# Token-major latent attention in layer 0, and a stage's first weight splits ordered behind its norm

## The chip, the cores and the metric

The kernel runs on one core of a Trainium2 chip. The metric is the time of one execution in device microseconds, smaller is better. A core has five engines with a queue each: TensorE (PE, with its weight loads as PEld), VectorE (DVE), ScalarE (ACT), GpSimd (POOL) and SyncE (SP, which here only issues DMA transfers). Every queue runs in order: an instruction that waits holds all that stands behind it on the same engine.

## The reference

Two transformer blocks, one after the other, each of two layers, on 256 tokens of width 1024, in float32. Layer 0 of the first block also carries 256 context tokens. Its mixer joins a gated delta-rule recurrence over both directions with a latent attention of 8 heads; the joined 1024 features go through `w_out`. Cut to what the change touches:

```python
mod = (jax.nn.silu(c) @ w_mod[i] + b_mod[i])[:, None, :]      # 6 x 1024 columns: shift, scale, gate, twice
...
def blocked_attention(q, k, v, scale):
    ...
        s = jnp.einsum('bqkgd,bskd->bkgqs', q_i, k).astype(jnp.float32) * scale
        p = jax.nn.softmax(s, axis=-1).astype(v.dtype)
        return jnp.einsum('bkgqs,bskd->bqkgd', p, v)
...
    b_lat = blocked_attention(q_l, jnp.concatenate([k_c, k_l], 1), jnp.concatenate([v_c, v_l], 1), scale)
    y_lat = jnp.concatenate([a_lat, b_lat.reshape(b, s_len, -1)], -1) @ w_out
...
h = h + gt_m * rms_norm(y, g_post_mix[i])
f = swiglu(modulate(rms_norm(h, g_pre_ffn[i]), sh_f, sc_f), w_ffn_gate[i], w_ffn_up[i], w_ffn_down[i])
```

The context tokens attend to the context alone, the others to context and tokens. The modulation is computed for `c` and for `c_ctx`.

## The kernel before, in words

**Products with weights.** Every large product is done in three passes of a split format: a float32 matrix is cut into a high part and a remainder, and `mm3` (L553 to L556) adds high by high, high by low and low by high. For a weight, `Weights.load` and its sisters issue a DMA of a `[128, 2, 512]` piece (two contraction tiles by up to 512 columns, 512 KB) into a raw buffer `wraw`; `Weights.cut` has ScalarE write the high part `whi` (L270), and VectorE or POOL subtract to the low part `wlo`, one instruction for each of the two contraction tiles (L272). Which of the two does it is set by `W.turn`: a string with a letter for each of the stage's loads, V for VectorE and P for POOL; `turn("PPPP", "V")` gives the first four loads to POOL and the rest to VectorE. Raw buffers and part buffers rotate; a load waits until its buffer is free.

**The order of the work.** The program is written stage by stage, but when the kernel is built a planner lays out each engine's queue: it walks through a model of time and places what has its operands and buffers, what comes earlier in the program first. So work of a later part may be placed in the gaps of an earlier one. Buffers of a ring, and the eight accumulation banks of TensorE, are given out by kind with a fixed count each.

**Layer 0's mixer** has the banks `g` (3), `s` (2), `tp`, `po` and `gv` (one each). After the projections come the recurrence (`gdn_run`, over 8 pairs of direction and token tile, each two chunks of 64 tokens; its `gQ` operands are loaded by SP at L1172, its state is updated by POOL at L1207), `gdn_post`, the attention (`l0_mla`), and last six modulation chunks (`mod_chunk` for n = 4 to 9):

```python
with Pool(K, "mla", "right"):
    l0_mla(K, Om)
    for n in range(4, 10):
        mod_chunk(K, W, K.po, 0, n)
```

A modulation chunk takes a `gv` bank, multiplies four loads of `w_mod` into it (L370 the loads, L373 sixteen matmul instructions, 32 columns wide), copies the result to a row `mrow` on ScalarE (L375), takes a `gv` bank again for a closing product (L379 where the section is a gate, L386 elsewhere) and adds the bias on VectorE. Gate sections fetch bias and gain and store the gate row through POOL's queue.

**The attention before** is feature-major. For each of four head pairs and four tiles of 128 query tokens, `attend` makes scores, takes the row maximum (L674), the exponential with its row sum (L676), transposes the probabilities on TensorE (L679) and copies them (L682, L684). The product with the values has the values as stationary operand (128 by 64) and the probabilities streaming (L690), so that the output has features on partitions. The softmax sums are per token; `sums_row` takes the reciprocal of the sums broadcast to 128x128 (L698) and turns it by a matmul into the bank `gv` (L700). After the four tiles, L872 copies that bank and L873 multiplies. In `layer0` the result is split by features (four 128x512 splits).

**Where a stage begins.** A stage ends in `post_norm`: squares, a reciprocal root by Newton steps on VectorE (L319 to L323), the residual (L542), for some stages a product with a row of gains (L546), squares of the new residual on ScalarE (L514), and then `norm_tile`: the scaled identity `ndg` (L507) and matmuls with it that give the next stage's features (L489; L487 where there is no scaling), which are then split (L306, L307). The next stage's first weights are loaded and split meanwhile.

Of the kernel before, what the change touches and what calls it, by code (L numbers as in the profile page):

```python
# [10 lines left out]
F32 = mybir.dt.float32  # L11
# [92 lines left out]
def const(K, n):  # L104
    pack, a, b = COFF[n]
    return K.cst[pack][:, a:b]


def setup(K, tc, ctx, ins, out):
    K.nc = tc.nc  # L110
    K.tc = tc
    K.ins = ins
    K.out = out
    K.n = 0
    K.sb = ctx.enter_context(tc.tile_pool(name="sb", bufs=1))
    K.cur = K.sb
    K.dr = ctx.enter_context(tc.tile_pool(name="dr", bufs=1, space=DRAM))
    K.cst = {}
    K.open = []
    K.np = K.nu = 2  # L120
    K.c = lambda n: const(K, n)

# [77 lines left out]
def bank(K, kind):  # L200
    kind = K.alias.get(kind, kind)
    return K.ps[kind].tile([128, 512], F32, name=nm(K, kind), tag=kind, bufs=K.kinds[kind])
# [14 lines left out]
class Weights:  # L217
# [9 lines left out]
    def turn(self, pattern, then=None):  # L227


        self.first = pattern if then else ""  # L230
        self.rest = then or pattern
        self.nt = 0

    def engine(self):
# [33 lines left out]
    def cut(self, raw, hi, lo):  # L268
        e = self.engine()
        self.K.nc.scalar.copy(hi, raw)  # L270
        for k in range(raw.shape[1]):
            e.tensor_tensor(lo[:, k], raw[:, k], hi.bitcast(F32)[:, k], op=ALU.subtract)  # L272

# [229 lines left out]
def norm_tile(K, x, ss, coef, hi, lo, t):  # L503


    dg = cut(K, [128, 128], F32, "ndg", 2)
    K.nc.vector.tensor_scalar_mul(dg, K.ident, rstd2(K, ss, "n"))  # L507
    to_features(K, x, coef, hi, lo, t, dg)


def squares(K, h, ss, q, tag="yj"):

    j = cut(K, [128, 512], F32, tag, 1)
    K.nc.scalar.activation(j, h[:, q * 512:q * 512 + 512], AF.Square, accum_out=ss[:, q:q + 1])  # L514


def post_norm(K, G, hdst, after, sq=True, T=2, row=None, held=True):
# [6 lines left out]
    def consume(c, t, ps):  # L524
# [9 lines left out]
        if c == 1:  # L534
            r = rstd2(K, ss, "p")
            s2 = cut(K, [128, 2], F32, "hss", 4)
            h = x = hdst(t)
            if row is not None:
                x = cut(K, [128, D], F32, "xn", 2)
            for q in range(2):  # L540
                cq = slice(q * 512, q * 512 + 512)
                nc.vector.scalar_tensor_tensor(h[:, cq], ys[t, q], r, h[:, cq], op0=ALU.mult, op1=ALU.add)  # L542
                if sq:
                    squares(K, h, s2, q)
                if row is not None:
                    nc.vector.tensor_tensor(x[:, cq], h[:, cq], row[:, cq], op=ALU.mult)  # L546
            return lambda: after(t, s2, x)
# [117 lines left out]
def attend(K, score, v, po, rb, c, kinds=("s", "s", "tp", "tp")):  # L665
# [22 lines left out]
    for j in range(nj):  # L688
        for hh in range(2):
            nc.tensor.matmul(po[hh * 64:hh * 64 + 64, c:c + 128], v(hh, j), pts[hh][0][:, j * 128:(j + 1) * 128],  # L690
                             start=(j == 0), stop=(j == nj - 1))


# [94 lines left out]
def l0_mla(K, O):  # L788
# [50 lines left out]
    for pair in range(4):  # L839
        heads = {}  # L840
        for h in (2 * pair, 2 * pair + 1):
# [17 lines left out]
            heads[h] = (q1, q2, k1, k2)  # L859
        po, rb = bank(K, "po"), bank(K, "gv")  # L860
        for t in range(4):
            n = 256 if t < 2 else 512

            def score(pss):
                tk = slice(t * 128, (t + 1) * 128)
                for hh in range(2):
                    q1, q2, k1, k2 = heads[2 * pair + hh]
                    mm3(K, pss[hh][:, :n], q1[:, tk], q2[:, tk], k1[:, :n], k2[:, :n], True, True)
                    yield pss[hh][:, :n]
            attend(K, score, lambda hh, j: vt[:, j, pair * 128 + hh * 64:pair * 128 + hh * 64 + 64], po, rb, t * 128,  # L870
                   ("s", "g", "tp", "g") if late else ("s", "s", "tp", "tp"))
        nc.scalar.copy(O[:, pair, :], rb)  # L872
        nc.vector.tensor_tensor(O[:, pair, :], po, O[:, pair, :], op=ALU.mult)  # L873

# [860 lines left out]
def ple(K, W, i, xh, xl, pp, h, after=None, out=None, fill=None, row=None):  # L1735
# [4 lines left out]
    def consume(c, t, ps):  # L1740
# [7 lines left out]
        else:  # L1748
            if t not in sss:
                sss[t] = cut(K, [128, 2], F32, "yss", 4)  # L1750
                xs[t] = cut(K, [128, D], F32, "xn", 2)
            squares(K, h[t], sss[t], c)
            nc.vector.tensor_tensor(xs[t][:, cs], h[t][:, cs], row[:, cs], op=ALU.mult)
# [112 lines left out]
def layer0(K):  # L1866
# [18 lines left out]
    with Banks(K, {"acc": 5, "aux": 2, "gv": 1}):  # L1885
        with Pool(K, "tmp"):
# [3 lines left out]
            gdn_out(K, mh[:, 0:4], ml[:, 0:4])  # L1890
            for k in range(4):
                split(K, mh[:, 4 + k], ml[:, 4 + k], Om[:, k])
            K.dbg("gh", mh[:, 0:4])
# [14 lines left out]
        with Pool(K, "ff"):  # L1908
            hT = cut(K, [128, 22, 512])
            W.turn("PPPP", "V")  # L1910
            with Pool(K, "sg"):
# [47 lines left out]
def layer1(K, h):  # L1959
    nc = K.nc  # L1960
    ins = K.ins
    W = K.W
    K.px = opened(K, "w", "right")
    W.add(K.px, 1, 2)
    with Pool(K, "l1o"):
        load_const(K, "rest", K.cur)
        oh, ol = cut(K, [128, 8, 256], FR), cut(K, [128, 8, 256], FR)
        W.turn("PPPPPP", "V")
        with mix_banks(K), Pool(K, "l1"):
# [22 lines left out]
    with Pool(K, "ff"):  # L1992
        mh, ml = cut(K, [128, 22, 256], FR), cut(K, [128, 22, 256], FR)
        W.turn("VVVVPPPP", "V")
        with Pool(K, "sg"):
# [20 lines left out]
def second(K, h):  # L2016
# [10 lines left out]
    for i in range(2):  # L2027
        with Pool(K, "so"):
# [4 lines left out]
            W.add(K.px, 1, 2)  # L2033
            W.turn("PPPP", "V")
            with mix_banks(K), Pool(K, "sU"):
# [21 lines left out]
        with Pool(K, "ff"):  # L2057
            mh, ml = cut(K, [128, 32, 256], FR), cut(K, [128, 32, 256], FR)
            W.turn("VVVVPPPP", "V")
            with Pool(K, "sg"):  # L2060
# [110 lines left out]
```

## Time before, and its profile

| | |
|---|---|
| Median of 3 runs | 2217.39 us (2213.5 to 2222.52) |
| The profiled execution: time | 2211.2 us |
| Its span, first to last instruction | 2209.4 us |
| Mean granted TensorE clock | 0.936 of full speed |

A granted clock of 1.0 is 2.4 GHz and 0.5 is 1.2 GHz. Busy times of the engines overlap, so shares do not add up to one. An idle engine costs time only where the others wait for it. In the rows below, a line of a group gives line, engine, operation, output and inputs, shapes and count, then busy us and mean ns of one, then the idle time ahead of it and what ended that; a line in order of time begins with the start in us and the duration.

### The profile page before, as it was taken

Reading aid. Unit: us, or ns where it says so; the run is one execution under the profiler, and the core shown is the slowest. Engines: PE = TensorE matmul, PEld = TensorE weight load, DVE = VectorE, ACT = ScalarE, POOL = GpSimd, SP = SyncE. Lnnn points to the kernel's source line nnn. Section 1 sums busy time; section 2 is a strip of 40 time slices with the busy share of each in tenths; the row PEclk is TensorE's granted clock in tenths of the full one; section 3 lists DMA queues with packets and bytes.
Section 4 is the critical chain, followed back from the end, with each engine's and each line's share of the span. In section 5 each row is a group of like instructions: output and inputs, shape, how many; then the busy total and the mean of one; then the engine's idle time right before and its main releaser. Section 6 shows DMA issues by size and latency. Waiting matters only on the chain.

```text
span 2209.4 us, 31163 instructions
## 1 busy us (share of the span) xinstructions
PE 2035.4 (92%) x11656; PEld 1640.6 (74%) x11656; DVE 1319.9 (60%) x2737; ACT 921.9 (42%) x1612; POOL 241.2 (11%) x312
## 2 busy tenths in 40 slices
PE   6989898857999999979987999999899999989998
PEld 3777677614887877867656888898688879868886
DVE  5665566702678674463856556585675467566644
ACT  4533433402522223443435544455454345545532
POOL 2211112100100000020311000210200021020000
PEclk9999599957999999989969999999899999989999
DMA  8343300155267663222304557350566535145561
GB/s 273 91 111 82 116 11 16 59 170 171 85 204 234 223 200 105 96 88 67 96 20 152 154 151 241 111 145 20 162 198 188 158 117 162 44 153 167 185 190 68
DMA packets 186952, 291.90 MB, mean 132 GB/s; under 512 B 28472, under 2 KB 75704, under 8 KB 186800
## 3 DMA queue, kind: packets, MB, share of 16 engines
q1 hardware_dynamic: 172720, 272.54, 39.6%
q0 software_dynamic: 5472, 16.13, 2.2%
q10 hardware_dynamic: 8608, 1.23, 0.4%
q8 instruction: 92, 1.51, 0.3%
q14 instruction: 60, 0.49, 0.1%
HBM read 281.44 MB, written 8.41 MB: 131 GB/s over the span
## 4 chain that ended last, share of the span: by engine, by line
PE 81%; DVE 6%; DMA 5%; issue 3%; ACT 3%; POOL 1%; SPq 0%; ACTq 0%; DVEq 0%; POOLq 0%
PE acc L554 18%; PE acc L556 18%; PE acc L555 18%; PE s L554 2%; PE s L555 2%; PE s L556 2%; PE gv L373 2%; DMA wraw<-in_w_mod_dram 2%; PE po L1531 1%; PE tp L1531 1%; PE po L690 1%; PE tp L891 1%; PE aux L729 1%; PE aux L489 1%; PE g L1200 1%
## 5 line engine op out<-in xcount | busy, mean ns | idle before, releaser
L272 DVE TENSOR_TENSOR wlo<-wraw,whi 128x512 fp32r<-128x512 f32 (+4 forms) x772 | 483.1, 669 | 301.2 <-ACT whi L270 284.4
L270 ACT CAST whi<-wraw 128x1024 fp32r<-128x1024 f32 (+4 forms) x420 | 413.6, 990 | 491.2 <-PE acc L556 204.2
L554 PE MATMUL acc<-whi,u 128*128 128x512 f32 (+3 forms) x1320 | 511.5, 390 | 21.5 <-ACT whi L270 13.2
L555 PE MATMUL acc<-wlo,u 128*128 128x512 f32 (+3 forms) x1320 | 509.4, 388 | 0.8 <-DVE wlo L272 0.7
L556 PE MATMUL acc<-whi,u 128*128 128x512 f32 (+3 forms) x1320 | 507.9, 386 | 1.5 <-DVE u L307 1.5
L554 PEld LDWEIGHTS acc<-whi,u 128*128 128x128 f32 x1320 | 253.2, 192 | 72.7 <-ACT whi L270 15.1
L556 PEld LDWEIGHTS acc<-whi,u 128*128 128x128 f32 x1320 | 252.6, 191 | 51.7 <-DVE u L307 3.8
L555 PEld LDWEIGHTS acc<-wlo,u 128*128 128x128 f32 x1320 | 252.7, 192 | 51.2 <-DVE wlo L272 3.6
L554 PE MATMUL acc<-u,whi 128*128 128x512 f32 (+1 forms) x480 | 169.5, 360 | 1.8 <-ACT u L306 1.7
L556 PE MATMUL acc<-u,wlo 128*128 128x512 f32 (+1 forms) x480 | 170.1, 358 | 0.0
L555 PE MATMUL acc<-u,whi 128*128 128x512 f32 (+1 forms) x480 | 169.4, 355 | 0.2 <-DVE u L307 0.2
L272 POOL TENSOR_TENSOR wlo<-wraw,whi 128x512 fp32r<-128x512 f32 (+1 forms) x68 | 83.7, 1261 | 417.4 <-ACT whi L270 417.4
L432 DVE SCALAR_TENSOR_TENSOR msum<-mraw,u,msum 128x512 f32<-128x512 f32 x140 | 100.7, 745 | 12.8 <-DMA mraw<-in_w_mod_dram 11.7
L554 PEld LDWEIGHTS acc<-u,whi 128*128 128x128 f32 x480 | 89.5, 189 | 16.9 <-issue 2.6
L555 PEld LDWEIGHTS acc<-u,whi 128*128 128x128 f32 x480 | 90.4, 188 | 15.2 <-issue 1.7
L556 PEld LDWEIGHTS acc<-u,wlo 128*128 128x128 f32 x480 | 90.1, 188 | 15.1 <-issue 1.7
L307 DVE TENSOR_TENSOR u<-aux,u 128x512 fp32r<-128x512 f32 (+2 forms) x96 | 59.4, 632 | 44.0 <-ACT u L306 44.0
L373 PE MATMUL gv<-wraw,u 128*32 128x512 f32 x160 | 50.2, 900 | 32.2 <-DMA wraw<-in_w_mod_dram 24.6
L306 ACT CAST u<-aux 128x512 fp32r<-128x512 f32 (+2 forms) x96 | 50.4, 543 | 55.7 <-PE aux L729 35.8
L554 PE MATMUL acc<-whi,dxh 128*128 128x512 f32 x176 | 69.7, 396 | 1.9 <-ACT dxh L306 1.9
L555 PE MATMUL acc<-wlo,dxh 128*128 128x512 f32 x176 | 69.6, 396 | 0.0
L556 PE MATMUL acc<-whi,dxl 128*128 128x512 f32 x176 | 69.0, 396 | 0.0
(510 smaller groups left out, 3115.2 us busy)
## 6 DMA issues: line engine op xcount, KB each, us to landing
wraw<-in_w_up_dram SPq DMA_DIRECT2D x64, 512.0 KB, 4.2
wraw<-in_w_down_dram SPq DMA_DIRECT2D x64, 512.0 KB, 4.3
mraw<-in_w_mod_dram SPq DMA_DIRECT2D x56, 512.0 KB, 4.8
wraw<-in_w_ffn_down_dram SPq DMA_DIRECT2D x44, 512.0 KB, 3.8
wraw<-in_w_mod_dram SPq DMA_DIRECT2D x40, 512.0 KB, 4.8
wraw<-in_w_ffn_gate_dram SPq DMA_DIRECT2D x48, 256.0 KB, 3.0
wraw<-in_w_ffn_up_dram SPq DMA_DIRECT2D x48, 256.0 KB, 3.3
wraw<-in_w_ffn_gate_dram SPq DMA_DIRECT2D x20, 512.0 KB, 4.3
```

Source lines behind the costliest of these rows:

```text
L270: self.K.nc.scalar.copy(hi, raw)
L272: e.tensor_tensor(lo[:, k], raw[:, k], hi.bitcast(F32)[:, k], op=ALU.subtract)
L306: (hi_eng or nc.scalar.copy)(hi, src)
L307: nc.vector.tensor_tensor(lo, src, hi.bitcast(F32), op=ALU.subtract)
L373: nc.tensor.matmul(ps[32 * j:32 * j + 32, :], K.cl[:, g + k, :], raw[:, k, :], start=(g + k < 4), stop=(g + k >= 4))
L432: nc.vector.scalar_tensor_tensor(accs[s], raw[:, k, :], c, accs[s], op0=ALU.mult, op1=ALU.add)
L489: nc.tensor.matmul(ps[:, k * 128:(k + 1) * 128], xk, dg, start=True, stop=True)
L554: mm(ps, ah, bh, start=start, stop=False)
L555: mm(ps, ah, bl, start=False, stop=False)
L556: mm(ps, al, bh, start=False, stop=stop)
L690: nc.tensor.matmul(po[hh * 64:hh * 64 + 64, c:c + 128], v(hh, j), pts[hh][0][:, j * 128:(j + 1) * 128], start=(j == 0), stop=(j == nj - 1))
L1531: nc.tensor.matmul(ps[t][:, c * 128:c * 128 + 128], yp[:, c, t * 128 + j:t * 128 + j + 128] if j < 31 else ones, dg, start=(j == 0), stop= ...
```

## The change

Two things are done. Layer 0's attention becomes token-major: a new `attend_tok` uses the transposed probabilities as stationary operand and the values as streaming one, scales the output by the reciprocal of the two sums per token, and writes it with tokens on partitions; `layer0` turns the four token tiles by `out_features` (transposes on TensorE, then a split). The banks `po` and `gv` are no longer held over a head pair; `gv` isn't used by the attention at all. And at seven stage starts the turns with POOL become VectorE throughout; in their place `W.wait` orders the first weights' casts behind the square (on ScalarE) and their subtractions behind the scaled identity or the last residual operation (on VectorE) of a token tile. These are edges for the planner within one engine; they add no semaphore wait. `{0: 0, 4: 2}` means: loads from the 0th on go behind tile 0, from the 4th on behind tile 2, up to four loads past the last key.

```diff
@@ class Weights
     def turn(self, pattern, then=None):
+        self.behind = {}
...
+    def wait(self, chains):
+        self.behind = {n: self.K.chain[t] for n, t in chains.items()}
+
+    def order_of(self, ins, n, i):
+        at = [m for m in self.behind if m <= n]
+        if at and n < max(self.behind) + 4:
+            self.K.tc.add_manual_dep(ins.ins, self.behind[max(at)][i].ins.name, mybir.DependencyInfo(
+                mybir.DependencyClass.NoSync, mybir.DependencyReason.DATA), reason="norm first")
...
     def cut(self, raw, hi, lo):
-        e = self.engine()
-        self.K.nc.scalar.copy(hi, raw)
+        n, e = self.nt, self.engine()
+        self.order_of(self.K.nc.scalar.copy(hi, raw), n, 1)
         for k in range(raw.shape[1]):
-            e.tensor_tensor(lo[:, k], raw[:, k], hi.bitcast(F32)[:, k], op=ALU.subtract)
+            i = e.tensor_tensor(lo[:, k], raw[:, k], hi.bitcast(F32)[:, k], op=ALU.subtract)
+            if e is self.K.nc.vector:
+                self.order_of(i, n, 0)
@@ norm_tile
-    K.nc.vector.tensor_scalar_mul(dg, K.ident, rstd2(K, ss, "n"))
+    K.chain[t][0] = K.nc.vector.tensor_scalar_mul(dg, K.ident, rstd2(K, ss, "n"))
@@ post_norm
+            K.chain[t] = [v, a]        # last VectorE operation on the residual, last square
@@ new
+def attend_tok(K, pair, t, score, v, O, kinds=("s", "s", "tp", "tp")):
+    nc = K.nc
+    sm = cut(K, [128, 2], F32, "sm", 4)
+    pts = []
+    for hh in range(2):
...
+    po = bank(K, "po")
+    for hh in range(2):
+        pt, nj = pts[hh]
+        for j in range(nj):
+            nc.tensor.matmul(po[:, hh * 64:hh * 64 + 64], pt[:, j * 128:(j + 1) * 128], v(2 * pair + hh, j),
+                             start=(j == 0), stop=(j == nj - 1))
+    r = cut(K, [128, 2], F32, "rs", 4)
+    nc.vector.reciprocal(r, sm)
+    nc.vector.tensor_tensor(O.rearrange("p (h d) -> p h d", h=2), po[:, :128].rearrange("p (h d) -> p h d", h=2),
+                            bc(r, [128, 2, 64], 2), op=ALU.mult)
@@ l0_mla
-        po, rb = bank(K, "po"), bank(K, "gv")
...
-            attend(K, score, lambda hh, j: vt[:, j, pair * 128 + hh * 64:pair * 128 + hh * 64 + 64], po, rb, t * 128,
-                   ("s", "g", "tp", "g") if late else ("s", "s", "tp", "tp"))
-        nc.scalar.copy(O[:, pair, :], rb)
-        nc.vector.tensor_tensor(O[:, pair, :], po, O[:, pair, :], op=ALU.mult)
+            attend_tok(K, pair, t, score, lambda h, j: vt[:, j, h * 64:(h + 1) * 64],
+                       O[:, t, pair * 128:(pair + 1) * 128], ("s", "g", "tp", "g") if late else ("s", "s", "tp", "tp"))
@@ layer0
-            for k in range(4):
-                split(K, mh[:, 4 + k], ml[:, 4 + k], Om[:, k])
+            for t in range(4):
+                out_features(K, Om[:, t, :], mh, ml, 4, t)
@@ layer0, FFN
-            W.turn("PPPP", "V")
+            W.turn("V")
+            W.wait({0: 2})
@@ layer1, mixer
-        W.turn("PPPPPP", "V")
+        W.turn("V")
+        W.wait({0: 0, 4: 2})
@@ layer1, FFN (and the second block's FFN, twice)
-        W.turn("VVVVPPPP", "V")
+        W.turn("V")
+        W.wait({0: 0, 6: 1})
@@ the second block's mixer, twice
-            W.turn("PPPP", "V")
+            W.turn("V")
+            W.wait({0: 0})
```

The scores, maxima, exponentials and transposes of `attend_tok` are those of `attend`. The two products of `ple_product` keep their turn on POOL.

## Rows read from the trace of the kernel before

**Rows 1.** The page's first part: busy time, share of the span and instructions of each engine.

```profile
PE 2035.4 (92%) x11656; PEld 1640.6 (74%) x11656; DVE 1319.9 (60%) x2737; ACT 921.9 (42%) x1612; POOL 241.2 (11%) x312
```

**Rows 2.** Busy time of each engine in three stretches of layer 0's mixer. Columns: stretch, its length, busy us and instructions of PE, PEld, DVE, ACT, POOL, then granted TensorE clock, DMA share and GB/s.

```profile
185.00:434.00 249.00, 220.93 (x2401) 180.63 (x2401) 154.01 (x330) 94.23 (x220) 48.27 (x75) 0.86 0.19 52
434.00:515.00 81.00, 48.57 (x150) 13.60 (x149) 9.41 (x19) 8.45 (x15) 4.78 (x9) 0.58 0.52 167
515.00:535.00 20.00, 12.47 (x31) 8.24 (x31) 8.62 (x14) 6.86 (x8) 2.96 (x2) 0.67 0.63 218
```

**Rows 3.** The matmuls of line 373 from 255 to 560 us (durations as minimum, median, maximum, then first and last start), and what ended TensorE's idle time ahead of them (us, times).

```profile
L373 PE MATMUL gv<-wraw,u x96: 592/1061/1062, 434.0 to 511.4; 128*32 128x512 f32 x96
...
  DMA wraw<-in_w_mod_dram: 61.5, 22
```

**Rows 4.** The loads of `w_mod` in SP's queue in order of time (line 370), from 60 to 560 us.

```profile
179.79 1.56 SPq L370 DMA_DIRECT2D wraw<-in_w_mod_dram  x2
...
435.05 70.88 SPq L370 DMA_DIRECT2D wraw<-in_w_mod_dram  x22
```

**Rows 5.** The instructions that write or read the bank `gv` from 60 to 434 us, the attention's only.

```profile
L700 PE MATMUL gv<-const_id,rs x32: 272/275/582, 301.5 to 432.7; 128*128 128x128 f32 x32
...
L872 ACT COPY u<-gv x4: 579/588/592, 321.2 to 433.0; 128x512 f32<-128x512 f32 x4
```

**Rows 6.** TensorE in order of time in the stretch after the attention, runs of one line merged: two loads' matmuls, one load's, and a closing product.

```profile
433.96 1.07 PE L373 MATMUL gv<-wraw,u 128*32 128x512 f32 x8
...
439.19 1.05 PE L373 MATMUL gv<-wraw,u 128*32 128x512 f32 x4 [3.15 <-DMA wraw<-in_w_mod_dram]
...
473.70 1.87 PE L386 MATMUL gv<-const_id,mrow 128*128 128x2 f32 x8 [0.73 <-ACT mrow L375]
```

**Rows 7.** DMA issues from 434 to 515 us: count, KB each, median us from issue to landing.

```profile
wraw<-in_w_mod_dram SPq DMA_DIRECT2D x22, 512.0 KB, 4.1
```

**Rows 8.** Groups of instructions from 280 to 450 us: operations of the attention that the change takes out.

```profile
L698 DVE RECIPROCAL rs<-sm 128x128 f32<-128x128 f32 x16 | 15.2, 952 | 4.5 <-ACT p L676 4.1
...
L700 PE MATMUL gv<-const_id,rs 128*128 128x128 f32 x32 | 7.2, 308 | 0.0
...
L873 DVE TENSOR_TENSOR u<-po,u 128x512 f32<-128x512 f32 x4 | 2.8, 692 | 1.5 <-ACT u L306 1.2 <-PE po L690 0.3
```

**Rows 9.** First, TensorE in order of time: the attention's value product and what follows it, and the same for the second block's attention, which has probabilities as stationary operand. Then the weight loads of both, the second block's scaling and reciprocal, and the transposes that bring a recurrence output back to features.

```profile
318.96 1.09 PE L690 MATMUL po<-pt,u 128*64 128x128 f32 x14
319.98 0.66 PE L679 MATMUL tp<-const_id,p 128*128 128x128 f32 x4
...
1545.85 1.00 PE L1660 MATMUL po<-u,pt 128*128 128x64 f32 x8
1546.69 0.39 PE L1655 MATMUL tp<-const_id,p 128*128 128x128 f32 x2
...
L690 PEld LDWEIGHTS po<-pt,u 128*64 128x64 f32 x192 | 13.2, 136 | 6.6 <-issue 3.4 <-ACT p L676 1.5 <-ACT pt L684 0.2
L1660 PEld LDWEIGHTS po<-u,pt x96: 186/192/337, 1539.3 to 1951.3; 128*128 128x128 f32 x96
L1664 DVE TENSOR_TENSOR u<-po,rs x16: 283/292/292, 1541.4 to 1951.7; 128x128 f32<-128x128 f32 x16
L1663 DVE RECIPROCAL rs<-asm x16: 154/166/168, 1515.6 to 1947.8; 128x2 f32<-128x2 f32 x16
L1253 PE MATMUL aux<-const_id,u 128*128 128x128 f32 x16 | 3.1, 353 | 0.0
```

**Rows 10.** The subtractions of line 272 in the whole kernel, shapes apart, on VectorE and on POOL.

```profile
L272 DVE TENSOR_TENSOR wlo<-wraw,whi 128x512 fp32r<-128x512 f32 x628 | 411.5, 698 | 246.4 <-ACT whi L270 231.3 <-POOL wlo L272 11.0 <-PE acc L556 2.5
L272 POOL TENSOR_TENSOR wlo<-wraw,whi 128x512 fp32r<-128x512 f32 x52 | 71.1, 1397 | 402.4 <-ACT whi L270 402.4
L272 DVE TENSOR_TENSOR wlo<-wraw,whi 128x256 fp32r<-128x256 f32 x56 | 21.3, 421 | 23.7 <-ACT whi L270 22.2 <-PE aux L1350 1.6
L272 POOL TENSOR_TENSOR wlo<-wraw,whi 128x256 fp32r<-128x256 f32 x16 | 12.7, 820 | 15.1 <-ACT whi L270 15.1
```

**Rows 11.** The product with the row of gains on VectorE, in order of time, two at a time: with POOL idle, and with POOL subtracting from 1577.6 to 1588.6 us.

```profile
1410.25 1.29 DVE L546 TENSOR_TENSOR xn<-u,u 128x512 f32<-128x512 f32 x2
...
1580.46 3.26 DVE L546 TENSOR_TENSOR xn<-u,u 128x512 f32<-128x512 f32 x2
```

**Rows 12.** The start of layer 1's FFN in order of time, on VectorE, ScalarE and TensorE: the residual, a weight's cast, the second square, and the first matmuls with the scaled identity.

```profile
1201.73 1.41 DVE L542 SCALAR_TENSOR_TENSOR u<-acc,rsy1p,u 128x512 f32<-128x512 f32 x2
...
1204.43 1.04 ACT L270 CAST whi<-wraw 128x1024 fp32r<-128x1024 f32 x1 [1.26 <-DMA wraw<-in_w_ffn_up_dram]
...
1206.94 0.62 ACT L514 ACTIVATE yj<-u 128x512 f32<-128x512 f32 x1
...
1211.42 3.75 PE L489 MATMUL aux<-ndg,u 128*128 128x128 f32 x16 [7.29 <-DVE ndg L507]
```

**Rows 13.** What TensorE waited for from 520 to 2210 us: us in total, times, longest us.

```profile
PE aux L489 <- DVE ndg L507: 15.1, 4, 7.3
...
PE aux L489 <- DVE rsy1p L323: 8.6, 1, 8.6
PE aux L487 <- DVE xn L546: 8.5, 6, 1.8
```

**Rows 14.** The chain that ended last, in order of time: the first load of the output projection's weights on it.

```profile
516.73 6.55 DMA wraw<-in_w_out_even_dram
```

More of the change, by code (lines that the diff above doesn't have):

```diff
@@ L120, in setup @@
     K.np = K.nu = 2
+    K.chain = {}
     K.c = lambda n: const(K, n)
@@ L513, in squares @@
     j = cut(K, [128, 512], F32, tag, 1)
-    K.nc.scalar.activation(j, h[:, q * 512:q * 512 + 512], AF.Square, accum_out=ss[:, q:q + 1])
+    return K.nc.scalar.activation(j, h[:, q * 512:q * 512 + 512], AF.Square, accum_out=ss[:, q:q + 1])
 def post_norm(K, G, hdst, after, sq=True, T=2, row=None, held=True):
@@ L541, in consume @@
                 cq = slice(q * 512, q * 512 + 512)
-                nc.vector.scalar_tensor_tensor(h[:, cq], ys[t, q], r, h[:, cq], op0=ALU.mult, op1=ALU.add)
-                if sq:
-                    squares(K, h, s2, q)
+                v = nc.vector.scalar_tensor_tensor(h[:, cq], ys[t, q], r, h[:, cq], op0=ALU.mult, op1=ALU.add)
+                a = squares(K, h, s2, q) if sq else None
                 if row is not None:
-                    nc.vector.tensor_tensor(x[:, cq], h[:, cq], row[:, cq], op=ALU.mult)
+                    v = nc.vector.tensor_tensor(x[:, cq], h[:, cq], row[:, cq], op=ALU.mult)
+            K.chain[t] = [v, a]
             return lambda: after(t, s2, x)
@@ L691, in attend @@
                              start=(j == 0), stop=(j == nj - 1))
+def attend_tok(K, pair, t, score, v, O, kinds=("s", "s", "tp", "tp")):
[3 more added lines that the diff above has]
+    for hh in range(2):
+        h = 2 * pair + hh
+        ps, nmx = score(h, t, bank(K, kinds[hh]))
+        n = ps.shape[-1]
+        if nmx is None:
+            nmx = cut(K, [128, 1], F32, "nmx", 6)
+            nc.vector.tensor_reduce(nmx, ps, axis=AX.X, op=ALU.max, negate=True)
+        p = cut(K, [128, 512], F32, "p", K.np)
+        nc.scalar.activation(p[:, :n], ps, AF.Exp, bias=nmx, accum_out=sm[:, hh:hh + 1])
+        tp = bank(K, kinds[2 + hh])
+        for j in range(n // 128):
+            nc.tensor.transpose(tp[:, j * 128:(j + 1) * 128], p[:, j * 128:(j + 1) * 128], K.ident)
+        pt = cut(K, [128, 512], F32, "pt", K.np)
+        if hh:
+            nc.vector.tensor_copy(pt[:, :n], tp[:, :n])
+        else:
+            nc.scalar.copy(pt[:, :n], tp[:, :n])
+        pts.append((pt, n // 128))
+    po = bank(K, "po")
[8 more added lines that the diff above has]
+                            bc(r, [128, 2, 64], 2), op=ALU.mult)
 def sums_row(K, sm, rb, c):
@@ L859, in l0_mla, with score @@
             heads[h] = (q1, q2, k1, k2)
-        po, rb = bank(K, "po"), bank(K, "gv")
         for t in range(4):
             n = 256 if t < 2 else 512
-            def score(pss):
+            def score(h, t, ps):
+                q1, q2, k1, k2 = heads[h]
                 tk = slice(t * 128, (t + 1) * 128)
[L866 to L869, printed above, removed]
-            attend(K, score, lambda hh, j: vt[:, j, pair * 128 + hh * 64:pair * 128 + hh * 64 + 64], po, rb, t * 128,
-                   ("s", "g", "tp", "g") if late else ("s", "s", "tp", "tp"))
-        nc.scalar.copy(O[:, pair, :], rb)
-        nc.vector.tensor_tensor(O[:, pair, :], po, O[:, pair, :], op=ALU.mult)
+                mm3(K, ps[:, :n], q1[:, tk], q2[:, tk], k1[:, :n], k2[:, :n], True, True)
+                return ps[:, :n], None
+            attend_tok(K, pair, t, score, lambda h, j: vt[:, j, h * 64:(h + 1) * 64],
+                       O[:, t, pair * 128:(pair + 1) * 128], ("s", "g", "tp", "g") if late else ("s", "s", "tp", "tp"))
 def gdn_conv(K, W, f0, nf, silu, tensor):
@@ L1751, in consume @@
                 xs[t] = cut(K, [128, D], F32, "xn", 2)
-            squares(K, h[t], sss[t], c)
+            K.chain[t] = [None, squares(K, h[t], sss[t], c)]
             nc.vector.tensor_tensor(xs[t][:, cs], h[t][:, cs], row[:, cs], op=ALU.mult)
@@ L2058, in second @@
             mh, ml = cut(K, [128, 32, 256], FR), cut(K, [128, 32, 256], FR)
-            W.turn("VVVVPPPP", "V")
+            W.turn("V")
+            W.wait({0: 0, 6: 1})
             with Pool(K, "sg"):
```

## The prediction

> **What bounds the kernel now.** I read the page first: TensorE is busy for 92% of the span [rows 1], so time can come only from fewer TensorE instructions, from stretches where it waits, or from stretches at the low clock. Next the table of stretches. Layer 0's mixer ends in two unlike parts: from 185 to 434 us TensorE works 220.9 of 249 us, and from 434 to 515 us only 48.6 of 81 us, at a granted clock of 0.58 instead of 0.86 [rows 2]. The reader should look at what the second part does. All 96 matmuls of the six modulation chunks (`mod_chunk`, n = 4 to 9) lie in it, the first at 434.0 us, and 22 times TensorE waits there for a `w_mod` load, 61.5 us in all [rows 3]. It is a stage that streams 24 half-megabyte loads through two buffers and does little else.
>
> Then the question why it stands there. Its first two loads were issued at 179.8 us; the other 22 only from 435 us on [rows 4]. So data lay ready for some 250 us. What was not free was its accumulator: `mod_chunk` takes the bank `gv`, of which there is one, and the attention holds that bank for the broadcast reciprocals of every head pair: L700 writes it from 301.5 to 432.7 us, and L872 starts to read it for the last time at 433.0 us, a copy of 0.59 us [rows 5]. The first chunk's matmul follows that copy's end by 0.4 us. Even before 301 us no chunk used it, though the loads were there: the first pair's tile comes earlier in the program and had the bank.
>
> Last, the starts of the later stages in the list of waits: TensorE's waits on VectorE's norm chain there are 15.1, 8.6 and 8.5 us [rows 13], 32 us in the whole kernel. That caps what the second half of the change can give, unless it also speeds up VectorE elsewhere.
>
> **Part one: attention token-major.** It removes 16 reciprocals over 128x128 (L698, 15.2 us of VectorE), the 32 matmuls of L700 (7.2 us of TensorE), L872 (four copies of 0.59 us on ScalarE [rows 5]) and L873 (2.8 us of VectorE) [rows 8]. It adds 16 reciprocals of 128x2 and 16 scalings of 128x128, priced by the same two operations of the second block, 0.166 and 0.29 us [rows 9]: 7.3 us. VectorE thus has 10.7 us less to do. On TensorE the probability-times-value product turns round. Before, 64 columns are loaded and 128 stream, two heads side by side: 14 instructions start within 1.02 us, 0.073 us each. The second block's product has the new shape and starts 8 in 0.84 us, 0.105 us each [rows 9]. For 192 instructions that is 6.1 us more. The transposes that bring four token tiles back to features cost as L1253's 16 instructions, 3.1 us [rows 9]; for 32, 6.2 us. TensorE: 6.1 + 6.2 - 7.2 = 5 us more. With one `po` bank, every product now also waits for the scaling before it, at most 16 x 0.46 = 7.4 us. I set the net at 0: the stretch has 28 us of TensorE idle [rows 2] and is tied by VectorE and ScalarE steps, which become shorter. Bounds: 11 us gained, 13 us lost.
>
> The rows price a 128-column weight load at 0.192 us (L1660) and a 64-column one at 0.136 us (L690), which supports a loss, not a doubling. The Trainium skill (TensorE: Matmul & The Clock Gate, LDWEIGHTS) says that a load's time goes by its columns, columns over 1.2 ns, so that 64 more columns would cost 53 ns, or 10.2 us over 192, and the end would come 4 us later than by my pitch; the spacing of the starts, not that rule, stands in the sum.
>
> What matters more is what the bank's release moves. Nothing else in this stage uses `gv`, so the six chunks can run, once the stage's projections have left the memory of their row buffers, in gaps of recurrence and attention. What moves, by queue: on SP 22 loads, which get in among the recurrence's `gQ` loads and wait for a raw buffer there, hence for TensorE; on POOL two rounds of bias, gain and gate-row transfers among the recurrence's state updates, which then queue behind a wait for L379; six 0.6 us row copies on ScalarE; small adds on VectorE. On TensorE the chunks' matmuls cost 1.0 us for two loads' together (433.96 us) and as much for one load's alone (439.19 us) [rows 6]: 12 to 24 us, I take 18; with six closing products (L386 takes 1.9 us at clock 0.58, so 1.1 us at full; L379 priced as that) 24 us. Of that I let half vanish in the 28 us of idle: 12 us on the path.
>
> Every chunk matmul placed in front of recurrence work makes that work wait if its load is late. Landing takes 4.1 us [rows 7]. If the load is always in time, the price is 0; if each of the 22 loads is awaited in full, 90 us. I take half a microsecond each, 11 us, nearer the low end, because two loads are under way at a time and the stretch moves almost nothing else (DMA share 0.19 [rows 2]).
>
> Behind the stage, the output projection now starts on loads issued at 509 us, after the chunks gave up the raw buffers, and its first waits are 6.6 us and a smaller one [rows 14]. With raw buffers free earlier these shrink: 0 to 11 us, I take 6. Left exposed is the last token tile's normalise, four transposes and split, about 4 us.
>
> Sum of part one: -81 + 12 + 11 + 4 - 6 + 0 = -60 us.
>
> **Part two: splits on VectorE behind the norm.** 60 of the 68 half-weight subtractions leave POOL (the two `ple_product` turns keep 8): 44 of 512 columns and 16 of 256, 1.40 and 0.82 us each on POOL, 0.70 and 0.42 us on VectorE [rows 10], so 37 us of VectorE work is added at seven starts, some 5 us each. Two gains stand against it. First, order: at layer 1's FFN start VectorE has made both halves of the norm's input by 1203.1 us; ScalarE first waits for a weight to convert at 1204.4 us, the second square starts only at 1206.9 us, and TensorE resumes at 1211.4 us after 7.3 us of idle [rows 12]. The new order puts the squares first: some 3 us there, less elsewhere. Second, contention: two multiplications of the row (L546) took 1.67 us each at the second block's FFN start, while POOL was subtracting, against 1.29 us for the pair at 1410 us, when POOL was idle [rows 11]: 2 us in one chain.
>
> The Trainium skill (SBUF — State Buffer, SBUF: two separate sides) says that VectorE and GpSimd take their shared ports by an exclusive lock, held for a whole instruction. The trace agrees in kind: a 0.65 us operation grew to 1.67 us beside 1.4 us ones. By full blocking the gain at each affected chain would be up to 2 us, as the rows already say.
>
> Against both stands that the first weights' low parts now come after the norm, when VectorE is also splitting the tokens. At six starts of 1.5 us gain each and one (layer 1, where TensorE idles longest) without any I put -8 us. Bounds: the 32 us of waits bound the gain, of which I allow 18 us, since the chain itself stays; the loss is bounded by the 37 us if nothing is covered, and I allow 10 us of it, as before every first matmul TensorE still has transposes to do.
>
> **Rivals.** *Forecast, 0.68:* chunks spread through recurrence and attention; 2211.2 - 60 - 8 = 2143 us for the profiled execution. The median of the runs shown is 6 us above that execution, so 2149 us; its own range is 2115 to 2175 us (everything at its better bound would give 49 us less than 2149, but not all at once).
>
> *Chunks only partly moved, or moved with waits, 0.14:* ahead of 434 us TensorE idles for just 28 us, and chunks come last in the program, so perhaps half of them stay behind the attention: 40 us of the stage remain and half of the 23 us is put back, -81 + 40 + 12 + 4 - 6 - 8 = -39, about 2178 us; if the moved half is also awaited for 1.8 us each, 2192 us.
>
> *The bank was not the gate, 0.10:* something else in the stack of pools holds the chunks, and the stage stays at 81 us. Against it: the short step from L872 to the first chunk. Time: part two and the shorter reciprocals alone, 2205 to 2217 us.
>
> *Splits uncovered, 0.04:* all 37 us of them on the path beside a full part one: 2217 - 60 + 37 = 2194 us.
>
> *Slower, 0.04:* the early chunks block the recurrence. At TensorE, SP and POOL alike the order is fixed, and a late load holds everything behind it. It decides once a load is awaited for more than (81 - 12 - 4 + 6 + 8) / 22 = 3.6 us on average; at the full 4.1 us the end is about 2217 + 11 = 2228 us.
>
> **The numbers.** The likeliest case gives 2149 us. The range of 2115 to 2192 us takes in the forecast nearly whole and the partial move. A measurement of this kernel can tell about 0.5%, 11 us. Faster by more: 0.68 + 0.14 + 0.04 and a third of the 0.10, so 0.89. Within: 0.07. Slower: 0.04.
>
> **What would show it.** Right: chunk matmuls (L373's successor) spread over the recurrence and done before the attention is; no stretch of 80 us at clock 0.58; the output projection's first matmul near 434 + 12 + 11 + 4 = 461 us; no VectorE operation beyond 1.3 us at the stage starts; TensorE's 7.3 us gap at layer 1's FFN start down to about 4. Wrong: the chunks still begin after the last attention product; `gQ` loads waiting in SP's queue behind `w_mod`; TensorE waiting for `wlo` at the starts of stages.

## The result and the profile after

The changed kernel takes 2155.94 us (median; 2148.72 to 2168.22 us), against 2217.94 us for the kernel before, measured beside it: a ratio of 0.9726, with a 95% interval of 0.9676 to 0.9776. The forecast was 2149 us, 2115 to 2192. The total fits, but not by the sum that led to it: the first half gave 81 us instead of the 60 written down, and the second half took 18 us instead of giving 8. That the two errors, of 21 and 26 us, nearly cancel is luck.

The profiled execution took 2148.72 us, with a span of 2146.9 us. First the page's line of TensorE, and three stretches of layer 0 in the columns of [rows 2], to lay beside [rows 1, 2].

```profile
PE 2001.8 (93%) x11640; PEld 1637.2 (76%) x11640; DVE 1332.2 (62%) x2809; ACT 917.0 (43%) x1608; POOL 169.6 (8%) x252
```

```profile
185.00:434.00 249.00, 225.27 (x2466) 178.78 (x2466) 147.90 (x354) 94.75 (x219) 52.70 (x84) 0.91 0.38 117
434.00:451.00 17.00, 13.96 (x88) 11.57 (x85) 10.45 (x20) 9.09 (x16) 0.00 (x0) 0.90 0.24 79
451.00:476.00 25.00, 24.72 (x114) 20.27 (x115) 15.65 (x41) 9.61 (x20) 0.00 (x0) 1.00 0.36 115
```

The stretch of 81 us at clock 0.58 is gone. The 249 us ahead of it now hold the matmuls of the six chunks as well, and TensorE is busy there for 4.3 us more than before, at a granted clock of 0.91 instead of 0.86; the attention ends 7 us later, at 441.2 us instead of 434.0. Next the chunks' matmuls (line 387, formerly 373) and what TensorE waited for ahead of them, from 100 to 560 us; and TensorE in order of time around the output projection.

```profile
L387 PE MATMUL gv<-wraw,u x96: 592/617/1062, 192.2 to 332.2; 128*32 128x512 f32 x96
...
  DMA wraw<-in_w_mod_dram: 9.0, 2
```

```profile
439.24 1.97 PE L736 MATMUL po<-u,pt 128*128 128x64 f32 x16
...
442.83 0.50 PE L568 MATMUL acc<-whi,u 128*128 128x512 f32 x1 [0.52 <-ACT u L320]
...
451.28 0.73 PE L568 MATMUL acc<-whi,u 128*128 128x512 f32 x2 [1.18 <-ACT whi L282]
```

All 96 run from 192 to 332 us, with two waits for loads where [rows 3] has 22. L736 is the attention's last value product. The output projection starts at 442.8 us (before: 514.9), and the scaled identity of the FFN's first token tile is written at 475.9 us (before: 557.0). So layer 0's mixer and projection gave 81 us, while the whole span fell by 62.5 us. About 19 us went back in later stages. The list of TensorE's waits from 450 us to the end, beside [rows 13], says of what kind they are; the second fence has the kernel before's line of the wait that grew.

```profile
PE acc L568 <- ACT u L320: 27.5, 11, 8.2
PE aux L503 <- DVE ndg L521: 11.9, 2, 6.4
PE aux L503 <- DVE rsy1p L337: 9.1, 1, 9.1
...
PE aux L501 <- DVE xn L559: 0.8, 1, 0.8
```

```profile
PE acc L554 <- ACT u L306: 9.2, 7, 3.2
```

The waits on the scaled identity shrank as meant (15.1 to 11.9 us; those on the product `xn` from 8.5 to 0.8; the one on `rsy1p` stayed, 8.6 and 9.1), but waits for the token tile's own split (L320, formerly L306) rose from 9.2 to 27.5 us.

### The profile page after: what moved, and what is told of

Same layout as the page of the kernel before. It is cut to its first block, busy times and chain, and to the rows that moved or that the text cites. A ratio compares the mean times of both kernels' runs of the same rounds, so it can differ in the third digit from the quotient of the medians.

```text
span 2146.9 us, 31108 instructions
## 1 busy us (share of the span) xinstructions
PE 2001.8 (93%) x11640; PEld 1637.2 (76%) x11640; DVE 1332.2 (62%) x2809; ACT 917.0 (43%) x1608; POOL 169.6 (8%) x252
## 4 chain that ended last, share of the span: by engine, by line
PE 86%; DVE 7%; ACT 3%; DMA 2%; issue 2%; POOL 0%; SPq 0%; ACTq 0%; DVEq 0%; POOLq 0%
PE acc L568 19%; PE acc L570 19%; PE acc L569 19%; PE s L568 2%; PE s L569 2%; PE s L570 2%; PE tp L937 2%; PE po L1577 1%; DVE wlo L284 1%; PE tp L1577 1%; PE gv L387 1%; PE aux L779 1%; PE aux L503 1%; PE g L1246 1%; ACT whi L282 1%
## 5 line engine op out<-in xcount | busy, mean ns | idle before, releaser
L284 DVE TENSOR_TENSOR wlo<-wraw,whi 128x512 fp32r<-128x512 f32 (+4 forms) x832 | 513.4, 662 | 292.3 <-ACT whi L282 285.4
L569 PEld LDWEIGHTS acc<-u,whi 128*128 128x128 f32 x480 | 90.8, 189 | 15.5 <-issue 1.7
L320 ACT CAST u<-aux 128x512 fp32r<-128x512 f32 (+2 forms) x100 | 52.2, 544 | 62.3 <-PE aux L779 41.6
L321 DVE TENSOR_TENSOR dxl<-u,dxh 128x1024 fp32r<-128x1024 f32 x22 | 26.7, 1224 | 54.3 <-ACT dxh L320 54.3
L546 DVE TENSOR_TENSOR acc<-acc,u 128x512 f32<-128x512 f32 x30 | 20.9, 697 | 57.5 <-ACT yj L545 57.5
```

The costliest lines, as they stand in the source:

```text
L284: i = e.tensor_tensor(lo[:, k], raw[:, k], hi.bitcast(F32)[:, k], op=ALU.subtract)
L320: (hi_eng or nc.scalar.copy)(hi, src)
L321: nc.vector.tensor_tensor(lo, src, hi.bitcast(F32), op=ALU.subtract)
L569: mm(ps, ah, bl, start=False, stop=False)
```

## Experiments

The theory after the two traces: the bank's release is nearly all of the gain and is worth more than 60 us; the splits on VectorE cost 14 to 19 us at the starts of later stages. Medians of the kernel before beside these runs: 2219.0, 2218.3 and 2219.5 us.

**Each half alone.** The first half alone keeps the turns of the kernel before, at all five places that set them:

```
-        W.turn("V")
-        W.wait({0: 0, 6: 1})
+        W.turn("VVVVPPPP", "V")
```

> The changed kernel with its first half alone: token-major attention, while the stage starts split the first weights as the kernel before did (GpSimd's turns, no ordering behind the norm). The prediction's steps (part one -60, part two -8): 2157 to 2164 us, slower than the changed kernel's 2156. Theory from the two traces (part one gave 82 us, and part two took some 14 to 19 us of it back): 2136 to 2142 us, faster than the changed kernel by 0.6 to 0.9%. Rival (part two does nothing, and the later stages lost by a stretch of low clock alone): 2154 to 2158 us.

Measured: 2137.91 us, ratio 0.9637 (0.9608 to 0.9667), 18 us faster than the whole change. The second half alone keeps the attention, bank and all, of the kernel before:

> The kernel before with the second half alone: splits of the first weights on VectorE, ordered behind the norm; feature-major attention kept, with its one gv bank held over each head pair. The prediction's steps: 2210 us (-8). Theory from the traces: 2230 to 2237 us (+13 to +19). Rival (part two does nothing): 2216 to 2220 us.

Measured: 2229.97 us, ratio 1.0043 (1.0021 to 1.0066). So part one is worth -81 us, and part two costs 11 us alone (0.4%) and 18 us on top of part one. The rival that part two does nothing falls; how much of its cost comes by way of a lower clock is taken up at the end.

**What of part one is the bank.** First the changed kernel with the bank held again:

```
+        rb = bank(K, "gv")
         for t in range(4):
...
+            nc.tensor.matmul(rb[:, t:t + 1], O[:, t, pair * 128:(pair + 1) * 128], K.c("one")[:, 1:2], start=True, stop=True)
+        nc.scalar.copy(cut(K, [128, 4], F32, "held", 2), rb[:, :4])
```

> The changed kernel, but each head pair of the token-major attention holds the gv bank as the kernel before did: after each token tile a one-column matmul writes into it, and a 128x4 copy reads it after the pair; the output does not use it. If the release of the bank is the gain (prediction and theory now), the six chunks return behind the attention, and the time to 2156 + 75 to 85 = 2230 to 2240 us, with all 96 chunk matmuls after the last attention product. If shorter attention steps are the gain, it stays at 2156 to 2165 us.

Measured: 2221.86 us, ratio 1.0022 (1.0002 to 1.0041): 66 us of the gain gone, a little less than expected. The chunks' matmuls from 255 to 560 us:

```profile
L387 PE MATMUL gv<-wraw,u x96: 589/1061/1063, 424.0 to 499.9; 128*32 128x512 f32 x96
...
  DMA wraw<-in_w_mod_dram: 58.4, 26
```

They are back behind the attention, which ends at about 424 us when no chunk runs beside it. Then the other way round, the kernel before with one word changed:

```
-        po, rb = bank(K, "po"), bank(K, "gv")
+        po, rb = bank(K, "po"), bank(K, "g")
```

> The kernel before with one word changed: the feature-major attention keeps its broadcast reciprocals in one of the three g banks instead of the one gv bank. All else is as before. If the bank is the whole of part one's gain and the token-major form gives nothing: 2138 to 2146 us. If the form gives about 8 us of its own (the changed kernel with the bank held stood 8 us below the kernel before with the second half alone): 2146 to 2154 us. If a g bank less slows the recurrence and scores: 2160 us or more.

Measured: 2150.66 us, ratio 0.9702 (0.9675 to 0.9729). Its chunks, from 100 to 560 us:

```profile
L373 PE MATMUL gv<-wraw,u x96: 592/617/1062, 193.0 to 332.8; 128*32 128x512 f32 x96
```

They lie where the changed kernel has them, with the old attention. So 69 us come from the name of a bank (2219.5 to 2150.7), and the token-major form adds 13 us (2150.66 to 2137.91).

**What the moved chunks cost.** The changed kernel with each moved chunk cut to one load and one matmul:

```
-    for g in range(0, 8, KG):
+    cut6 = n > 3
+    for g in range(0, KG if cut6 else 8, KG):
...
+        if cut6:
+            nc.tensor.matmul(ps, K.ident, raw[:, 0, :], start=True, stop=True)
+            continue
```

> The changed kernel with most of the six moved chunks left out: each has one load and one matmul instead of four loads and sixteen matmuls, and keeps its closing products, copies and row transfers (the modulation values of layer 0's later half are then not those of the reference). It prices what the chunks cost where they now stand. The prediction's steps (12 us of matmuls and 11 us of waits on the path): 2156 - 20 = 2136 us. If they now run in TensorE's gaps: 2150 to 2156 us.

Measured: 2151.40 us, ratio 0.9694 (0.9666 to 0.9722), 4.5 us below the whole change. The trace is sharper: the output projection starts at 434.18 us instead of 442.83, and the lead is 9.6 us at 545 us; it is lost in later stretches at low clock that cutting chunks does not touch. So three quarters of the moved loads and most of the matmuls cost about 9 us where they stand. That is not the whole cost of the move, since the closing products, row copies, transfers and one load of each chunk are left in. The whole of it is read from the end of the attention in four traces: bank held or free, old form or new. The kernel before with the bank renamed ends its attention here:

```profile
452.78 1.09 PE L690 MATMUL po<-pt,u 128*64 128x128 f32 x14
```

| end of the attention's last value product, us | chunks behind it | chunks moved |
| --- | --- | --- |
| feature-major | 434.0 | 453.9 |
| token-major | 422.4 | 441.2 |

The move puts 19 to 20 us on the attention's end, near the forecast's 23 of matmuls and waits, and the token-major form takes 12 to 13 us off it, as by the medians. Each entry is one execution: seven more kernels with the token-major form and moved chunks end between 438.3 and 442.1 us, and the second half alone, feature-major with the bank held, ends at 439.6, so the move may have cost as little as 14 us.

From 240 to 300 us, in the columns of [rows 2], this kernel and then the changed one:

```profile
240.00:300.00 60.00, 59.04 (x951) 49.63 (x951) 37.02 (x121) 32.80 (x71) 9.85 (x27) 0.70 0.34 101
```

```profile
240.00:300.00 60.00, 54.47 (x932) 39.65 (x931) 35.93 (x118) 30.22 (x66) 10.34 (x28) 0.83 0.48 159
```

With the chunks in place TensorE is granted 0.83 in this stretch, without them 0.70 (the kernel before: 0.67; the changed kernel with the bank held: 0.76; the old attention with the chunks moved: 0.74). Part of what the chunks cost may so have been given back by the clock; how much, no run shows.

**What of part two costs: the engine or the order.** The changed kernel without its `W.wait` lines:

> The changed kernel with all turns on VectorE, but without the ordering of the first weights' casts and splits behind the norm's squares and scaling. If the ordering is what costs (casts and splits stand between the scaling and the token tile's own split): 2137 to 2146 us. If the engine is what costs (8 splits on VectorE at each start, wherever they stand): 2155 to 2170 us. By the prediction's steps the order gives most of part two's gain: 2158 to 2162 us.

Measured: 2158.93 us, ratio 0.9728 (0.9702 to 0.9755): over the whole kernel the order is worth nothing that can be told. By place it is worth something: counted from layer 1's last attention product to the 700th matmul into an `acc` bank behind it, the unordered kernel takes 5.2 us more than the first half alone and the ordered one 0.4. The ordered one loses 1 us at layer 1's mixer start, where the unordered one gains 1. And the order with the turns of the kernel before:

> The kernel with the first half alone (2138 us), plus the ordering: casts of the first weights behind the squares, and those splits that VectorE has behind the scaling, while GpSimd keeps its turns. The prediction's steps (the order gains 3 us at layer 1's FFN start and less elsewhere): 2132 to 2135 us. If the order is neutral, as between the two VectorE kernels (2156 and 2159): 2136 to 2140 us. If casts behind the squares come late for TensorE: 2142 to 2150 us.

Measured: 2141.29 us, ratio 0.9662 (0.9630 to 0.9694), the same as the first half alone within its interval. Over the four kernels (order or not, VectorE or turns with POOL) the loss goes with the engine: moving the splits to VectorE costs 15 us with the order (2141.29 to 2155.94) and 21 without (2137.91 to 2158.93).

**Where.** The second half undone at three of the seven starts, and its complement:

> The changed kernel with the second half undone at three of its seven starts, the FFN starts of layer 1 and of the two later layers: there GpSimd again takes the fifth to the eighth weight of the pattern, unordered; the other four starts keep splits on VectorE behind the norm. Theory (VectorE paces the FFN starts, where 4 weights of two 0.70 us splits each are 5.6 us more, 17 us at three starts; the other starts have room): 2138 to 2142 us. Rival (each of the seven starts loses its share of the 18 us): 2146 to 2150 us. Rival (the prediction's gain of order exists and lies at layer 1's FFN start): 2156 or more.

> The complement: the second half at those three FFN starts alone, GpSimd's turns at the other four. Theory (three FFN starts pay it all): 2152 to 2157 us. Rival (equal shares): 2145 to 2148 us.

Measured: 2147.82 us (0.9648 to 0.9715) and 2152.06 us (0.9661 to 0.9732). Over the first half alone that is 10 and 14 us, where the theory had 0 and 18 and equal shares 8 and 10. Neither is excluded by the medians. The same instructions timed in two traces say more. Against the first half alone, the second kernel loses 6.2 us from the second block's last attention product to the first residual behind its FFN, 4.9 us in the third FFN's, and, counted as above, 0.3 us at layer 1. The first loses 2 us at layer 1's mixer start; for the rest its profiled execution (2143.79 us) is faster than that of the first half alone (2145.99), so the two traces can't show where its 10 us by the medians are. What the other four starts cost stays open.

VectorE in order of time at the second block's FFN start, in the first half alone: splits (L284), the residual of token tile 0 (L556), the product with the row (L559), and tile 1's residual.

```profile
1508.37 1.29 DVE L284 TENSOR_TENSOR wlo<-wraw,whi 128x512 fp32r<-128x512 f32 x2 [0.54 <-ACT whi L282]
...
1512.26 1.29 DVE L284 TENSOR_TENSOR wlo<-wraw,whi 128x512 fp32r<-128x512 f32 x2
...
1513.65 1.28 DVE L284 TENSOR_TENSOR wlo<-wraw,whi 128x512 fp32r<-128x512 f32 x2
...
1516.21 1.41 DVE L556 SCALAR_TENSOR_TENSOR u<-acc,rsy1p,u 128x512 f32<-128x512 f32 x2
1517.54 3.27 DVE L559 TENSOR_TENSOR xn<-u,u 128x512 f32<-128x512 f32 x2
...
1526.94 1.41 DVE L556 SCALAR_TENSOR_TENSOR u<-acc,rsy1p,u 128x512 f32<-128x512 f32 x2
```

The same in the changed kernel:

```profile
1508.11 0.70 DVE L546 TENSOR_TENSOR acc<-acc,u 128x512 f32<-128x512 f32 x1 [6.05 <-ACT yj L545]
...
1510.81 1.41 DVE L556 SCALAR_TENSOR_TENSOR u<-acc,rsy1p,u 128x512 f32<-128x512 f32 x2
1512.14 1.28 DVE L559 TENSOR_TENSOR xn<-u,u 128x512 f32<-128x512 f32 x2
...
1514.12 1.29 DVE L284 TENSOR_TENSOR wlo<-wraw,whi 128x512 fp32r<-128x512 f32 x2
...
1515.45 1.28 DVE L284 TENSOR_TENSOR wlo<-wraw,whi 128x512 fp32r<-128x512 f32 x2
...
1516.84 2.49 DVE L284 TENSOR_TENSOR wlo<-wraw,whi 128x512 fp32r<-128x512 f32 x4
...
1519.96 1.28 DVE L321 TENSOR_TENSOR u<-aux,u 128x512 fp32r<-128x512 f32 x2
...
1522.06 2.49 DVE L284 TENSOR_TENSOR wlo<-wraw,whi 128x512 fp32r<-128x512 f32 x4
...
1526.33 1.41 DVE L556 SCALAR_TENSOR_TENSOR u<-acc,rsy1p,u 128x512 f32<-128x512 f32 x2
```

In the first half alone the splits fill VectorE's time ahead of tile 0's residual, and tile 1's follows 10.7 us behind it (11.0 us in the kernel before, 1579.14 to 1590.17). In the changed kernel VectorE idles 6.05 us ahead of tile 0, because its splits are held back, and then does twelve of them, 7.55 us, between the two tiles: 15.5 us from residual to residual. Tile 0 is early, and tile 1 is late.

Without the order, the same splits stand ahead of tile 0 instead. The changed kernel without `W.wait`, the operation ahead of tile 0's reciprocal root (L546) and the two residuals:

```profile
1516.94 0.70 DVE L546 TENSOR_TENSOR acc<-acc,u 128x512 f32<-128x512 f32 x1 [1.91 <-ACT yj L545]
...
1528.04 1.41 DVE L556 SCALAR_TENSOR_TENSOR u<-acc,rsy1p,u 128x512 f32<-128x512 f32 x2
...
1535.90 1.41 DVE L556 SCALAR_TENSOR_TENSOR u<-acc,rsy1p,u 128x512 f32<-128x512 f32 x2
```

Counted in us from the end of the second block's last attention product:

| | tile 0's residual | tile 1's residual | first residual behind the FFN |
| --- | --- | --- | --- |
| kernel before | 25.6 | 36.6 | 217.9 |
| first half alone | 25.4 | 36.1 | 216.1 |
| the same turns at this start, other starts changed | 26.4 | 37.3 | 218.0 |
| first half, with the order | 22.9 | 36.0 | 217.1 |
| changed kernel | 24.1 | 39.6 | 222.7 |
| changed kernel without the order | 32.3 | 40.2 | 221.9 |

The order decides only whether tile 0 is late. With the splits on VectorE tile 1 comes 2 to 4 us later either way, and the residual behind the FFN 4 to 7 us later. Kernels with the same turns here differ by 2 us.

**Less on VectorE still.** If VectorE is what paces these starts, taking splits off it should pay:

```
-        W.turn("VVVVPPPP", "V")
+        W.turn("PPPPPPPP", "V")
```

> The kernel with the first half alone (2138 us), but at the three FFN starts GpSimd takes the first four weights of the pattern too, so that VectorE has 5.6 us less to do at each. If VectorE's time there lies wholly on the path in either direction: 2138 - 3 x 5.6 = 2121 us. If GpSimd becomes the late one (eight weights of two 1.40 us splits are 22 us in a row): 2138 to 2150 us, with TensorE waiting for wlo.

Measured: 2133.47 us, ratio 0.9621 (0.9591 to 0.9651), 4 us below the first half alone, which the intervals don't separate. By the traces it is 1.8 and 0.9 us ahead over the two later FFNs and loses 3.5 us at layer 1's. VectorE at the second block's start:

```profile
1506.85 1.41 DVE L556 SCALAR_TENSOR_TENSOR u<-acc,rsy1p,u 128x512 f32<-128x512 f32 x2
1508.17 3.02 DVE L559 TENSOR_TENSOR xn<-u,u 128x512 f32<-128x512 f32 x2
...
1517.17 1.41 DVE L556 SCALAR_TENSOR_TENSOR u<-acc,rsy1p,u 128x512 f32<-128x512 f32 x2
```

The contention that part two was to remove is there in full (3.02 us for the pair, 1.28 alone), and yet the tiles follow each other in 10.3 us. Against the turns of the kernel before, the 5.6 us taken off VectorE gain far less than they cost when they are put on it. Keeping this at the two later starts alone:

> The kernel with the first half alone, but at the FFN starts of the two later layers GpSimd takes the first eight weights of the pattern, and at layer 1's FFN start, where the trace of the run with all three on GpSimd lost 3.6 us, the turns are those of the kernel before. By the traces, 2 us gained at each of the two starts: 2133 us; by the medians, 4 us of the run with all three kept and 3.6 us more: 2130 us. If it is only scatter: 2138 us.

Measured: 2135.66 us, ratio 0.9635 (0.9610 to 0.9660). With the same turns at the two later FFNs as the run above, this one is level with the first half alone there (0.2 and 0.1 us behind), so the 1.8 and 0.9 us are scatter. The three kernels from 2133 to 2138 us can't be told apart; each is about 1% faster than the change as made, and 81 to 85 us faster than the kernel before.

## Why the prediction was right, and where it was not

| step | forecast | measured |
| --- | --- | --- |
| the stage behind the attention goes | -81 | gone |
| put back: chunk matmuls 12, late loads 11 | +23 | +19 (14 to 20) |
| put back: last token tile | +4 | +2 |
| output projection starts on loads that are there | -6 | -9 |
| the attention's own operations | 0 | -12 to -13 |
| part one | -60 | -81 |
| part two | -8 | +18 (alone +11) |

**The gate, right.** The bank `gv` held the chunks; one word in the kernel before frees them, and holding it again brings them back. The two rivals that doubted this (the chunks moved in part, or held by something else) fall, as does the slower one: loads were awaited twice, 9.0 us in all, not 3.6 us each.

**The matmuls and waits put back, nearly right.** The sum had 23 us; the attention's end moved by 19 to 20 us when the chunks moved ahead of it. Eleven us of waits were assumed, half a microsecond for each of 22 loads; TensorE waited 9.0 us, in two waits. In the new place the chunks' 96 matmuls take a median of 617 ns, against 1061 ns [rows 3], and the stretch around them is granted 0.91 instead of 0.86. That the output projection starts only 72 us earlier, not 81, so that 9 us seem to have come back, is the net of this cost, of the last tile's 1.6 us and of the next term.

**The attention's own operations, mis-sized.** This is the term that failed in part one. Set at 0 with a gain of at most 11 us; the two runs that differ in the form alone put it at 13 us, and the attention's end moves by 12 to 13 us. That shorter VectorE and ScalarE steps between matmuls counted for more than TensorE's 5 us of extra work is likely; no run takes these apart.

**The output projection, nearly right.** From its first matmul to the first scaled identity it takes 33.1 us instead of 42.1; -9 where -6 was written. The prediction read a wait of 6.6 us from a load on the chain [rows 14]; TensorE's own waits for casts of these weights were 4.3 and 2.8 us, and are 1.2 us now. The rest goes with a granted clock of 0.95 instead of 0.83 in the two stretches.

**Part two, wrong in sign.** Its mechanisms all happened: the squares come first, the pair of row products fell from 3.26 [rows 11] to 1.28 us, and the trace agrees with what the prediction took from the Trainium skill (SBUF — State Buffer, SBUF: two separate sides) in that the operation shrank once POOL's subtractions had gone. At layer 1's FFN start the norm's chain is faster. TensorE, then VectorE and ScalarE there, and last the first product in the kernel before:

```profile
1137.82 0.80 PE L568 MATMUL acc<-whi,u 128*128 128x512 f32 x1 [8.22 <-ACT u L320]
```

```profile
1122.44 1.41 DVE L556 SCALAR_TENSOR_TENSOR u<-acc,rsy1p,u 128x512 f32<-128x512 f32 x2
...
1126.91 0.29 DVE L521 TENSOR_SCALAR ndg<-const_id,rsy1n 128x128 f32<-128x128 f32 x1
1127.12 4.90 DVE L284 TENSOR_TENSOR wlo<-wraw,whi 128x512 fp32r<-128x512 f32 x8
...
1132.53 0.41 DVE L510 TENSOR_SCALAR u<-aux,u 128x128 f32<-128x128 f32 x1
```

```profile
1132.15 1.04 ACT L282 CAST whi<-wraw 128x1024 fp32r<-128x1024 f32 x1 [1.75 <-DMA wraw<-in_w_ffn_up_dram]
1134.37 1.04 ACT L282 CAST whi<-wraw 128x1024 fp32r<-128x1024 f32 x1 [1.17 <-DMA wraw<-in_w_ffn_up_dram]
...
1137.15 1.14 ACT L320 CAST u<-u 128x512 fp32r<-128x512 f32 x2 [1.03 <-DVE u L510]
```

```profile
1216.22 0.50 PE L554 MATMUL acc<-whi,u 128*128 128x512 f32 x1 [1.05 <-ACT u L306]
```

The scaling is written at 1126.91 us, 4.5 us behind the residual (9.4 in the kernel before, from 1201.73 to 1211.09 us), and then 4.90 us of weight splits stand on VectorE ahead of the token tile's affine step (L510), while ScalarE waits for two late weights ahead of the token's cast (L320). The first product comes 15.4 us behind the residual; before, 14.5. TensorE's idle time did not shrink to 4 us but moved, from 7.3 us ahead of the scaled identity to 8.2 us ahead of the first product. Here gain and loss cancel: the FFN is 0.4 us behind the first half alone. At the two later FFN starts the loss stays, 6.6 and 4.7 us.

The step that failed is the cover: the prediction counted 37 us of VectorE work, named the moment (VectorE then also splits the tokens), and let the transposes hide all but a little of it. At the starts the path runs on behind the scaling, through the token's affine and split and through the next tile's residual, on VectorE itself. The bound it wrote, 10 us of loss, was below the 18 measured on top of part one (11 alone). The rival with all 37 us uncovered overshot.

## What to carry over

Before moving instructions to another engine behind a critical step, follow the path past that step: the time bought at one instruction is lost if the next link of the path stands on the same engine behind the moved work. A contended operation (1.28 us grown to 3.0) can cost less than the 5.6 us that removing the contention brings onto the engine that paces the stage. And when a stage stands late in program order with its data long loaded, look for the buffer or bank that it shares: renaming one bank gave 69 us here without any other change.

## What the runs showed that was not expected

The time of one kernel follows its mean granted clock closely: in the six executions of the first half alone it goes from 2145.99 us at 0.950 to 2129.92 us at 0.959. Two traces show one place where that happens, layer 1's mixer from 1040 to 1097 us, in two kernels that are the same up to there (the first half alone, and the one with GpSimd's turns at the three FFN starts):

```profile
1040.00:1097.00 57.00, 50.74 (x247) 33.49 (x246) 25.54 (x38) 19.20 (x45) 0.37 (x1) 0.65 0.06 19
```

```profile
1040.00:1097.00 57.00, 49.58 (x312) 32.69 (x310) 30.77 (x45) 22.92 (x54) 0.20 (x1) 0.82 0.06 19
```

The second does 312 matmuls in that time, the first 247, and it is 8.7 us ahead at the end. So the difference of two spans misleads here: by the profiled spans (2144.2 and 2146.9 us) part two would cost 3 us; the medians say 18, and executions at the same mean clock of 0.950 (2145.99 and 2153.68 us) 8. How much of the other 10 us is a lower clock that part two's waits bring about, and how much is scatter between executions, these runs don't settle.
